# One kernel, one change: the chunks of the mLSTM and of the retention, and the RWKV gram matrices, put out in smaller steps

## The chip, the core and the metric

The kernel runs on one core of one Trainium2 chip. The metric is the device time of one execution in microseconds (us), the median of several runs; the profile shows one further execution, taken by the hardware profiler. Engines are named as in the profile: PE is TensorE (PEld its weight loads), DVE VectorE, ACT ScalarE, POOL GpSimd, and SP the engine whose queue issues the DMA transfers.

## What is computed

One layer over 1024 frames of width 1024, all in float32: an RMS norm, one input projection, three groups of heads side by side, an output projection, a second norm with a SwiGLU feed-forward part, and a last norm.

```python
def reference(x, w_in, ...):
    for l in range(DEPTH):                      # DEPTH = 1
        h = rmsnorm(x, ln1_g[l])
        p = h @ w_in[l]
        pm, pr, pw = jnp.split(p, [M_COLS, M_COLS + R_COLS], axis=-1)
        ym = mlstm_group(pm, ...)               # 4 heads of 64
        yr = retention_group(pr)                # 6 heads of 64
        yw = rwkv7_group(pw, ...)               # 6 heads of 64
        y = jnp.concatenate([ym, yr, yw], axis=-1).astype(x.dtype)
        x = x + y @ w_out[l]
        h = rmsnorm(x, ln2_g[l])
        x = x + (jax.nn.silu(h @ w_gate[l]) * (h @ w_up[l])) @ w_down[l]
    return rmsnorm(x, lnf_g)
```

mLSTM and retention are linear attention with decay, computed chunk by chunk. Within a chunk the scores (keys times queries), weighted by a causal decay mask, multiply the values; the state of the chunks before multiplies the queries; both are added, and the state takes in the chunk's keys and values. RWKV-7 is a recurrence with a delta rule, worked here in blocks of 64 frames: each block needs products of its decayed keys and queries with each other (the gram matrices), the inverse of a triangular matrix, and then a step of a serial chain.

## The kernel before

**Tiling.** Channels lie on 128 partitions, frames in two halves of 512 (h = 0, 1). A float32 projection is made from three products of split operands (a high and a low part, type fp32r), so each weight tile costs three matmuls, 512 frames wide in `three` (L119 to L121) or 256 columns wide in `tok_proj` (L740 to L742). The page calls those results `acc`. Weights come by DMA (`wraw`), and ACT and DVE split them (L90, L93). The small work, in plain float32, uses three PSUM buffers called `misc`; the RWKV chain has two of its own called `chain`.

**The woven stage.** Everything between the input projection and the first half of the output projection is written as Python generators, and `weave` decides in which order their instructions are put out. Each generator yields `(cost, wait)`: the planner's clock moves on by `cost`, and that generator is due again `wait` later; or it yields the name of an event and is due when another generator has signalled it. At each turn the first generator in the list that is due runs up to its next yield. The side work stands first in the list: `rwkv_chain`, `rwkv_inverse`, `rwkv_prep`, `rwkv_out`, `norms`, `attention`. The dense work stands behind: `rwkv_proj`, `fillers`, `out_proj`. So projections fill the time in which no side work is due, in quarters of a tile (`PART`, 1.38 planned us) or halves of a token tile (`TOK` x 256, 1.44). Side work is tied behind the last dense matmul put out before it (`tc.issue_after`); a dense matmul may still be drawn ahead of side work that the compiler's scheduler thinks not ready. PE then takes its instructions in the order that results.

**attention** (L1111 on) runs the eight chunks of 128 frames of the mLSTM, then four and four of the retention, one after another in one generator, each half of retention after its projections (`qkv_r0`, `qkv_r1`). For each chunk it puts out the whole of `mlstm_chunk` (L878) or `ret_chunk` (L947) in one step, then the loads of the next chunk, yields `(4.2, 4.0)` or `(5.0, 4.0)`, puts out the next mLSTM weights (POOL adds the mask at L873, ACT takes four exponentials at L876), stores the retention chunk before (L1007, 0.4 planned us), puts out the normalization of this chunk (`head_norm`), and waits 4.0 more. At the end of a half it signals `mlstm0`, `ret0` and so on; `norms` waits for them before `out_proj` can start on that half.

**A chunk of the mLSTM**: scores (L887), their product with the weights on DVE (L890), state times queries (L896) and weights times values (L898) for each of two head groups q, their sum (L901, L902), transposed keys (L908) scaled on DVE (L910), and the new state (L916, L922).

**A chunk of the retention**: queries and keys transposed (L953) and copied by ACT (L955), scores (L963); for each q the causal mask on DVE (L967, tile `rsw`), state times queries (L973), masked scores times values (L977), a scaling on DVE (L979); then the new state (L986, L989). The store transposes the result (L1007) and splits it.

**The grams** in `rwkv_half`: two passes of 16 matmuls (L466), four blocks each, every pass into two `misc` buffers that DVE empties with three masked products per buffer (L472 to L474). Behind them the step signals `ab` for the triangular inverse and yields `(2.2, 4.0)`.

**The RWKV chain** (L588 to L607) advances 48 blocks one after another, three steps each, with ACT and DVE between them, and ends with a normalization and a transposition (L655).

Of the kernel before, what the change touches and what calls it, by code (L numbers as in the profile page):

```python
# [54 lines left out]
def trunk_kernel(ctx: ExitStack, tc: tile.TileContext, a: dict, out: bass.AP):  # L55
# [16 lines left out]
    def misc_tile():  # L72
        return ps_m.tile([P, HF], F32, name="misc", tag="misc")
# [11 lines left out]
    def cc(name):  # L85
        lo, hi = CST[name]
        return cst[:, lo:hi]
# [101 lines left out]
    def rows_of(q):  # L189
        return slice(q * 64, (q + 1) * 64)  # L190
# [196 lines left out]
    def rwkv_half(i, h, r, k, v):  # L387
# [66 lines left out]
        for q in range(2):  # L454
            rows = rows_of(q)
# [5 lines left out]
        for c0 in range(0, 8, 4):  # L461
            grams = [misc_tile().rearrange("p (c x) -> p c x", c=4) for _ in two]
            for c in range(4):
                for q, g4 in enumerate(grams):
                    rows = rows_of(q)
                    PE.matmul(g4[:, c, :], lhsT=kb[rows, c0 + c, :, :].rearrange("p a t -> p (a t)"),  # L466
                              rhs=E[rows, c0 + c, q, 128:256], start=True, stop=True)
            for q, g4 in enumerate(grams):
                rows, orow = rows_of(q), rows_of(1 - q)
                cs4 = slice(c0, c0 + 4)  # L470
                msk = cc("mask_k").unsqueeze(1).broadcast_to([P, 4, 64])
                V.tensor_tensor(E[orow, cs4, q, 192:256], g4[rows, :, 0:64], msk[rows], ALU.mult)  # L472
                V.tensor_tensor(E[orow, cs4, q, 128:192], g4[orow, :, 0:64], msk[orow], ALU.mult)
                V.tensor_tensor(E[:, cs4, q, 64:128], g4[:, :, 64:128],  # L474
                                cc("mask_r").unsqueeze(1).broadcast_to([P, 4, 64]), ALU.mult)
        dl = sb.tile([P, 8], F32, name="dl", tag="dl", bufs=3)
        G.tensor_copy(dl, er[:, :, 64])
        inv = rwkv_inverse_issue(i, h, E)
        hv_E[i, h] = E, inv
        signal(f"ab{i}{h}", 3.0)  # L480
        yield 2.2, 4.0
        V.tensor_tensor(kb, kb, er[:, :, 64:65].unsqueeze(3).broadcast_to([P, 8, 2, 64]), ALU.mult)
        for c0 in range(0, 8, 4):
            pt = misc_tile()
# [393 lines left out]
    def mlstm_chunk(c, qT, kT, MV, ws):  # L878
        h2, sl = chunk_of(c)
        og = a_tile("og", 256)  # L880
        SY.dma_start(out=og, in_=v_dram[h2][sl, 256:512])
        hh = a_tile("hh", 260).rearrange("p (h d) -> p h d", h=4)
        scores = [misc_tile() for _ in two]
        for p in range(2):
            for q, pss in enumerate(scores):
                rows = rows_of(q)
                PE.matmul(pss[:, p * P:(p + 1) * P], lhsT=kT[rows, p, :], rhs=qT[rows, p, :], start=True, stop=True)  # L887
        for q, pss in enumerate(scores):
            rows = rows_of(q)
            V.scalar_tensor_tensor(ws[q], in0=pss[:, 0:256].rearrange("p (a b) -> p a b", a=2), scalar=0.125, in1=ws[q],  # L890
                                   op0=ALU.mult, op1=ALU.mult)
            po = misc_tile()
            p4 = po[:, 0:260].rearrange("p (w a e) -> p w a e", w=2, a=2)
            if c:
                for p in range(2):
                    PE.matmul(p4[:, 1, p, :], lhsT=qT[rows, p, :], rhs=CS["t"][rows, p, :], start=True, stop=True)  # L896
            for p in range(2):
                PE.matmul(p4[:, 0, p, :], lhsT=ws[q][:, p, :], rhs=MV[:, 2 * p + q, :], start=True, stop=True)  # L898
            dst = hh[:, q::2, :]
            if c:  # L900
                V.tensor_tensor(dst, p4[:, 1], mg["iw"][:, c, q::2].unsqueeze(2).broadcast_to([P, 2, 65]), ALU.mult)  # L901
                V.tensor_tensor(dst, dst, p4[:, 0], ALU.add)  # L902
            else:
                V.tensor_copy(dst, p4[:, 0])
        if c < KT - 1:
            pk = misc_tile()
            for p in range(2):
                PE.transpose(out=pk[:, p * P:(p + 1) * P], in_=kT[:, p, :], identity=ident)  # L908
            ks = a_tile("mks", 256).rearrange("p (h d) -> p h d", d=64)
            V.tensor_tensor(ks, pk[:, 0:256].rearrange("p (h d) -> p h d", d=64),  # L910
                            mg["sw"][:, c, :].unsqueeze(2).broadcast_to([P, 4, 64]), ALU.mult)
            pc = misc_tile()
            p3 = pc[:, 0:130].rearrange("p (a e) -> p a e", a=2)
            for p in range(2):
                for q in range(2):
                    PE.matmul(p3[rows_of(q), p, :], lhsT=ks[:, 2 * p + q, :], rhs=MV[:, 2 * p + q, :], start=True, stop=True)  # L916
            nw = at.tile([P, 2, 65], F32, name="CS", tag="CS", bufs=2)
            if c == 0:
                S.copy(out=nw, in_=p3)
            else:  # L920
                for p in range(2):
                    V.scalar_tensor_tensor(nw[:, p, :], in0=CS["t"][:, p, :], scalar=mg["decr"][:, c, p:p + 1],  # L922
                                           in1=p3[:, p, :], op0=ALU.mult, op1=ALU.add)
            CS["t"] = nw
        return hh, og
# [21 lines left out]
    def ret_chunk(c, qt, kt, RV):  # L947
        h2, sl = chunk_of(c)
        qkT = []
        for z in (qt, kt):  # L950
            pk = misc_tile()
            for p in range(3):
                PE.transpose(out=pk[:, p * P:(p + 1) * P], in_=z[:, p * P:(p + 1) * P], identity=ident)  # L953
            zT = a_tile("rT").rearrange("p (k t) -> p k t", k=3)
            S.copy(out=zT, in_=pk[:, 0:384].rearrange("p (k t) -> p k t", k=3))  # L955
            qkT.append(zT)
        qT, kT = qkT
        y = a_tile("ry").rearrange("p (h d) -> p h d", d=64)
        scores = [misc_tile() for _ in two]
        for p in range(3):  # L960
            for q, pss in enumerate(scores):
                rows = rows_of(q)
                PE.matmul(pss[:, p * P:(p + 1) * P], lhsT=kT[rows, p, :], rhs=qT[rows, p, :], start=True, stop=True)  # L963
        for q, pss in enumerate(scores):
            rows = rows_of(q)
            sw = a_tile("rsw").rearrange("p (a t) -> p a t", a=3)
            V.scalar_tensor_tensor(sw, in0=cc("causal").unsqueeze(1).broadcast_to([P, 3, P]), scalar=1.0,  # L967
                                   in1=pss[:, 0:384].rearrange("p (a j) -> p a j", a=3), op0=ALU.is_lt, op1=ALU.mult)
            po = misc_tile()
            p3 = po[:, 0:192].rearrange("p (a e) -> p a e", a=3)  # L970
            if c:
                for p in range(3):
                    PE.matmul(p3[:, p, :], lhsT=qT[rows, p, :], rhs=RR["t"][rows, p, :], start=(p == 0), stop=False,  # L973
                              skip_group_check=True)
            for p in range(3):
                hd = 2 * p + q
                PE.matmul(p3[:, p, :], lhsT=sw[:, p, :], rhs=RV[:, hd * 64:hd * 64 + 64], start=(c == 0), stop=True,  # L977
                          skip_group_check=True)
            V.tensor_tensor(y[:, q::2, :], p3, cc("qdec")[:, q::2].unsqueeze(2).broadcast_to([P, 3, 64]), ALU.mult)  # L979
        if c < KT - 1:  # L980
            pr = misc_tile()
            p3 = pr[:, 0:192].rearrange("p (a e) -> p a e", a=3)
            for p in range(3):
                for q in range(2):
                    hd = slice((2 * p + q) * 64, (2 * p + q) * 64 + 64)
                    PE.matmul(p3[rows_of(q), p, :], lhsT=kt[:, hd], rhs=RV[:, hd], start=True, stop=True)  # L986
            nw = at.tile([P, 3, 64], F32, name="RR", tag="RR", bufs=2)
            if c:
                V.tensor_tensor(nw, p3, RR["t"], ALU.add)  # L989
                V.tensor_tensor(nw, nw, cc("cdec").unsqueeze(2).broadcast_to([P, 3, 64]), ALU.mult)  # L990
            else:
                V.tensor_tensor(nw, p3, cc("cdec").unsqueeze(2).broadcast_to([P, 3, 64]), ALU.mult)
            RR["t"] = nw
        return (y,)
# [116 lines left out]
    def attention():  # L1111
# [2 lines left out]
                with late(G):  # L1114
                    mlstm_weights(t, args[-1])

        mlstm = ("mlstm", 4.2, mlstm_load, mlstm_chunk, mlstm_finish, None)
        ret = ("ret", 5.0, ret_load, ret_chunk, ret_finish, ret_store)
        for (name, cost, load, chunk, finish, store), start, ts in (
            (mlstm, "qkv_m", range(KT)), (ret, "qkv_r0", range(4)), (ret, "qkv_r1", range(4, KT)),  # L1120
        ):
# [3 lines left out]
            weigh(ts.start, args)  # L1125
            yield 0.0, 2.0
            for t in ts:
                y = chunk(t, *args)
                if t < ts.stop - 1:
                    args = load(t + 1)  # L1130
                yield cost, ATT
# [451 lines left out]
```

## Time and profile before

| What | us |
|---|---|
| median of 3 runs | 1495.96 |
| lowest and highest | 1495.2, 1502.91 |
| the profiled execution | 1500.5 |
| its span, from the first to the last instruction | 1498.7 |
| mean granted clock of PE over the span | 0.961 |

PE is the busiest engine. A page's row of a group gives its line, engine and operation, the tiles written and read, its count, its busy time and the mean of one, and the idle time of that engine in front of it with what ended that. A wait is written `engine line <- releaser: us in total, times, longest`. A matmul's busy time overlaps the next one's, so the distance of two starts tells more of its price than its duration.

### The profile page before, as it was taken

Reading aid. Unit: us, or ns where it says so; the run is one execution under the profiler, and the core shown is the slowest. Engines: PE = TensorE matmul, PEld = TensorE weight load, DVE = VectorE, ACT = ScalarE, POOL = GpSimd, SP = SyncE. Lnnn points to the kernel's source line nnn. Section 1 sums busy time; section 2 is a strip of 40 time slices with the busy share of each in tenths; the row PEclk is TensorE's granted clock in tenths of the full one; section 3 lists DMA queues with packets and bytes.
Section 4 is the critical chain, followed back from the end, with each engine's and each line's share of the span. In section 5 each row is a group of like instructions: output and inputs, shape, how many; then the busy total and the mean of one; then the engine's idle time right before and its main releaser. Section 6 shows DMA issues by size and latency. Waiting matters only on the chain.

```text
span 1498.7 us, 23112 instructions
## 1 busy us (share of the span) xinstructions
PE 1418.3 (95%) x8434; PEld 1152.0 (77%) x8434; DVE 885.4 (59%) x1763; ACT 547.5 (37%) x1179; POOL 436.2 (29%) x539
## 2 busy tenths in 40 slices
PE   7998998989989989999999999999999998999996
PEld 5777777878767878887777888888888887887886
DVE  7458585677756756745478555555555574347334
ACT  7353344223323243234545233333333344224222
POOL 3211122345333232424264443333434420000000
PEclk9999999989988999989999999999999999999998
DMA  5132232343522344463442222222222138336333
GB/s 201 51 131 68 63 100 78 93 118 109 131 66 63 106 119 138 119 184 109 158 169 85 78 85 85 85 85 84 82 69 76 70 128 290 99 95 239 95 98 113
DMA packets 131461, 165.33 MB, mean 110 GB/s; under 512 B 44532, under 2 KB 80532, under 8 KB 130196
## 3 DMA queue, kind: packets, MB, share of 16 engines
q1 hardware_dynamic: 131348, 163.87, 34.7%
q8 instruction: 66, 1.08, 0.3%
q14 instruction: 47, 0.39, 0.1%
HBM read 126.06 MB, written 37.77 MB: 109 GB/s over the span
## 4 chain that ended last, share of the span: by engine, by line
PE 71%; DVE 8%; DMA 8%; issue 3%; POOL 2%; ACT 2%; SPq 1%; DVEq 0%; POOLq 0%; ACTq 0%
PE acc L1193 5%; PE acc L1195 5%; PE acc L1194 5%; PE chain L1383 5%; PE chain L1382 5%; PE chain L1384 5%; PE acc L119 4%; PE misc L1193 4%; PE misc L1195 4%; PE misc L1194 4%; PE acc L121 4%; PE acc L120 3%; PE acc L740 2%; PE acc L741 2%; PE acc L742 2%
## 5 line engine op out<-in xcount | busy, mean ns | idle before, releaser
L93 DVE TENSOR_TENSOR wlo<-wraw,whi 128x512 fp32r<-128x512 f32 (+1 forms) x210 | 148.5, 713 | 138.0 <-ACT whi L90 131.8
L90 ACT ACTIVATE whi<-wraw 128x512 fp32r<-128x512 f32 (+1 forms) x210 | 128.2, 613 | 244.9 <-PE chain L1383 123.5
L90 ACT ACTIVATE whi<-rg 128x512 fp32r<-128x512 f32 x128 | 79.7, 631 | 225.3 <-POOL rg L1254 90.5
L119 PE MATMUL acc<-act,whi 128*128 128x512 f32 x352 | 152.3, 433 | 8.6 <-ACT whi L90 8.4
L740 PE MATMUL acc<-whi,act 128*128 128x256 f32 (+1 forms) x512 | 153.5, 304 | 4.4 <-ACT whi L90 3.9
L93 DVE TENSOR_TENSOR wlo<-rg,whi 128x512 fp32r<-128x512 f32 x128 | 94.5, 739 | 106.6 <-ACT whi L90 106.6
L741 PE MATMUL acc<-wlo,act 128*128 128x256 f32 (+1 forms) x512 | 151.4, 296 | 3.3 <-DVE wlo L93 3.3
L121 PE MATMUL acc<-act,wlo 128*128 128x512 f32 x352 | 146.5, 417 | 2.9 <-DVE wlo L93 2.9
L742 PE MATMUL acc<-whi,act 128*128 128x256 f32 (+1 forms) x512 | 149.3, 292 | 0.0
L1382 PE MATMUL chain<-act,whi 128*128 128x512 f32 (+1 forms) x374 | 144.3, 386 | 3.7 <-ACT act L90 3.7
L120 PE MATMUL acc<-act,whi 128*128 128x512 f32 x352 | 145.4, 414 | 1.4 <-DVE act L258 1.4
L1383 PE MATMUL chain<-act,whi 128*128 128x512 f32 (+1 forms) x374 | 143.9, 385 | 0.5 <-DVE act L93 0.5
L1384 PE MATMUL chain<-act,wlo 128*128 128x512 f32 (+1 forms) x374 | 143.8, 385 | 0.0
L1193 PE MATMUL acc<-act,whi 128*128 128x512 f32 x352 | 140.1, 398 | 2.8 <-ACT pre L1449 2.8
L1194 PE MATMUL acc<-act,whi 128*128 128x512 f32 x352 | 139.4, 396 | 0.0
L1195 PE MATMUL acc<-act,wlo 128*128 128x512 f32 x352 | 139.4, 396 | 0.0
L740 PEld LDWEIGHTS acc<-whi,act 128*128 128x128 f32 x512 | 99.1, 195 | 10.9 <-ACT whi L90 4.7
L741 PEld LDWEIGHTS acc<-wlo,act 128*128 128x128 f32 x512 | 100.1, 195 | 8.4 <-DVE wlo L93 4.5
L1193 PE MATMUL misc<-act,whi 128*128 128x512 f32 x264 | 104.2, 395 | 0.0
L1194 PE MATMUL misc<-act,whi 128*128 128x512 f32 x264 | 103.7, 393 | 0.0
L1195 PE MATMUL misc<-act,wlo 128*128 128x512 f32 x264 | 103.6, 393 | 0.0
L742 PEld LDWEIGHTS acc<-whi,act 128*128 128x128 f32 x512 | 100.0, 195 | 1.6 <-issue 0.3
(326 smaller groups left out, 2825.8 us busy)
## 6 DMA issues: line engine op xcount, KB each, us to landing
wraw<-in_w_down SPq DMA_DIRECT2D x85, 256.0 KB
rg<-in_w_gate SPq DMA_DIRECT2D x22, 512.0 KB
rg<-in_w_up SPq DMA_DIRECT2D x22, 512.0 KB
wraw<-in_w_tm SPq DMA_DIRECT2D x40, 256.0 KB
a_dram<-work SPq DMA_DIRECT2D x39, 256.0 KB
rg<-a_dram SPq DMA_DIRECT2D x9, 1024.0 KB
v_dram<-vt SPq DMA_DIRECT2D x64, 128.0 KB
wraw<-in_w_out SPq DMA_DIRECT2D x32, 256.0 KB
```

The lines of the kernel that those rows point to most:

```text
L90: S.activation(hi, src, AF.Copy, scale=scale)
L93: (eng or V).tensor_tensor(lo, src, hi.bitcast(F32), ALU.subtract)
L119: PE.matmul(ps, lhsT=hi, rhs=xh[:, k, :], start=(k == 0), stop=False)
L740: PE.matmul(o, lhsT=xh[h][:, k, sl], rhs=w[k][0], start=(k == 0), stop=False)
L741: PE.matmul(o, lhsT=xh[h][:, k, sl], rhs=w[k][1], start=False, stop=False)
L742: dense[0] = PE.matmul(o, lhsT=xl[h][:, k, sl], rhs=w[k][0], start=False, stop=(k == KT - 1)).ins
L1193: PE.matmul(ps, lhsT=hi, rhs=hi_x[:, k, :], start=(start and k == 0), stop=False, skip_group_check=True)
L1194: PE.matmul(ps, lhsT=hi, rhs=lo_x[:, k, :], start=False, stop=False, skip_group_check=True)
L1195: PE.matmul(ps, lhsT=lo, rhs=hi_x[:, k, :], start=False, stop=(stop and k == 3), skip_group_check=True)
L1382: PE.matmul(ps, lhsT=hi, rhs=hi_a[:, sl], start=(f == 0), stop=False)
L1383: PE.matmul(ps, lhsT=hi, rhs=lo_a[:, sl], start=False, stop=False)
L1384: PE.matmul(ps, lhsT=lo, rhs=hi_a[:, sl], start=False, stop=(f == FT - 1))
```

## The change

Nothing of the computation changes. `mlstm_chunk` and `ret_chunk` become generators that the attention generator runs with `yield from`: they yield between the scores and the values, before the state, and so on. The planned cost that attention adds after a chunk drops to 1.0. In `ret_chunk` both masked scores are now made before the first product with values. The grams yield once between their two passes. The loads of the next chunk come where they came, after the chunk's last instruction.

```diff
             if c0 == 0:
+                yield 1.1, 0.5
...
-        yield 2.2, 4.0
+        yield 1.1, 4.0
```

In `mlstm_chunk`:

```diff
         for q, pss in enumerate(scores):
-            rows = rows_of(q)
             V.scalar_tensor_tensor(ws[q], in0=pss[:, 0:256].rearrange("p (a b) -> p a b", a=2), scalar=0.125, in1=ws[q],
                                    op0=ALU.mult, op1=ALU.mult)
+        yield 0.8, 1.4
+        for q in range(2):
+            rows = rows_of(q)
             po = misc_tile()
...
         if c < KT - 1:
+            yield 1.8, 0.5
             pk = misc_tile()
...
                             mg["sw"][:, c, :].unsqueeze(2).broadcast_to([P, 4, 64]), ALU.mult)
+            yield 0.3, 1.2
             pc = misc_tile()
```

In `ret_chunk`:

```diff
         qT, kT = qkT
+        yield 0.8, 1.8
         y = a_tile("ry").rearrange("p (h d) -> p h d", d=64)
...
-        for q, pss in enumerate(scores):
-            rows = rows_of(q)
+        sws = []
+        for pss in scores:
             sw = a_tile("rsw").rearrange("p (a t) -> p a t", a=3)
             V.scalar_tensor_tensor(sw, in0=cc("causal").unsqueeze(1).broadcast_to([P, 3, P]), scalar=1.0,
                                    in1=pss[:, 0:384].rearrange("p (a j) -> p a j", a=3), op0=ALU.is_lt, op1=ALU.mult)
+            sws.append(sw)
+        for q, sw in enumerate(sws):
+            yield 1.2, 1.4
+            rows = rows_of(q)
             po = misc_tile()
...
         if c < KT - 1:
+            yield 1.2, 0.5
             pr = misc_tile()
```

In `attention`:

```diff
-        mlstm = ("mlstm", 4.2, mlstm_load, mlstm_chunk, mlstm_finish, None)
-        ret = ("ret", 5.0, ret_load, ret_chunk, ret_finish, ret_store)
+        mlstm = ("mlstm", 1.0, mlstm_load, mlstm_chunk, mlstm_finish, None)
+        ret = ("ret", 1.0, ret_load, ret_chunk, ret_finish, ret_store)
...
-                y = chunk(t, *args)
+                y = yield from chunk(t, *args)
```

More of the change, by code (lines that the diff above doesn't have):

```diff
@@ L475, in rwkv_half @@
                                 cc("mask_r").unsqueeze(1).broadcast_to([P, 4, 64]), ALU.mult)
+            if c0 == 0:
+                yield 1.1, 0.5
         dl = sb.tile([P, 8], F32, name="dl", tag="dl", bufs=3)
```

## The prediction

> **What bounds the kernel now.** I read the page first: the span, the busy shares and the chain that ended last.
>
> ```profile
> span 1498.7 us, 23112 instructions
> PE 1418.3 (95%) x8434; PEld 1152.0 (77%) x8434; DVE 885.4 (59%) x1763; ACT 547.5 (37%) x1179; POOL 436.2 (29%) x539
> PE 71%; DVE 8%; DMA 8%; issue 3%; POOL 2%; ACT 2%; SPq 1%; DVEq 0%; POOLq 0%; ACTq 0%
> ```
>
> TensorE bounds it: 95% busy, 71% of the chain. So an edit is worth what it takes out of PE's idle time, or what it changes in PE's speed. Next, the windows by stage (columns: length, then busy time of PE, PEld, DVE, ACT, POOL, then granted clock).
>
> ```profile
> 0.00:90.00 90.00, 77.81 (x344) 57.49 (x345) 53.87 (x84) 47.34 (x79) 26.93 (x44) 0.98 0.36 125
> 90.00:646.00 556.00, 513.22 (x4168) 426.72 (x4166) 369.61 (x1005) 190.99 (x540) 168.38 (x309) 0.94 0.35 100
> 646.00:746.00 100.00, 97.46 (x727) 74.16 (x728) 49.74 (x103) 46.71 (x126) 36.14 (x45) 0.93 0.45 146
> 746.00:1498.70 752.70, 729.80 (x3201) 593.61 (x3199) 412.19 (x573) 262.44 (x435) 204.74 (x141) 0.98 0.34 111
> ```
>
> The change lives between 90 and 746 us, the woven stage. PE is idle there for 556.0 - 513.2 + 100.0 - 97.5 = 45.3 us, and its clock is 0.94 and 0.93 against 0.98 elsewhere. That is the whole stock. The waits of PE in that stretch say whose it is (columns: total us, times, longest).
>
> ```profile
> PE chain L604 <- ACT X L600: 6.4, 4, 5.3
> PE misc L977 <- DVE rsw L967: 3.9, 2, 2.4
> PE misc L887 <- DMA mq<-mqk_dram: 2.9, 1, 2.9
> PE misc L655 <- POOL yw L851: 2.5, 1, 2.5
> PE misc L466 <- DVE R L528: 1.6, 1, 1.6
> PE misc L466 <- DVE E L474: 1.2, 1, 1.2
> PE misc L973 <- DVE gate L659: 0.8, 1, 0.8
> PE misc L898 <- DVE w L890: 0.6, 1, 0.6
> ```
>
> **Term 1: the waits inside the chunks and grams.** The rows that stand in front of the touched lines are L977, L466 twice, L973 and L898: 3.9 + 1.6 + 1.2 + 0.8 + 0.6 = 8.1 us. L604 and L887 are an RWKV copy and a load; the change moves neither. What such a wait looks like, in the third retention chunk:
>
> ```profile
> 598.53 0.94 PE L963 MATMUL misc<-rT 64*128 64x128 f32 x12
> 599.30 0.78 PE L973 MATMUL misc<-RR,rT 64*128 64x64 f32 x6
> 600.48 0.28 PE L740 MATMUL acc<-whi,act 128*128 128x256 f32 x1
> 602.56 0.55 DVE L967 SCALAR_TENSOR_TENSOR rsw<-cst,misc 128x384 f32<-128x384 f32 x1
> 603.17 0.88 PE L977 MATMUL misc<-rv,rsw 128*128 128x64 f32 x6 [2.41 <-DVE rsw L967]
> 603.98 1.36 PE L973 MATMUL misc<-RR,rT 64*128 64x64 f32 x6
> ```
>
> Scores, a few projection matmuls that slipped in, then PE stands 2.41 us because VectorE, busy with other work, reaches the mask only at 602.56. The change puts 1.2 + 1.4 planned us after the scores of retention and 0.8 + 1.4 after those of the mlstm; the same wait then lies under projection matmuls, a quarter of a tile (1.38 us) or half a token tile (1.44 us) at a time. The grams' second pass needs buffers that VectorE frees (L474); one projection step now stands between the passes. A wait that lasts longer than its cover still shows. I take the 8.1 us as gained; bounds 3 (only the waits up to 1.4 us go: 1.2 + 0.8 + 0.6) and 8.1. A VectorE late by more than that becomes the next wait.
>
> **Term 2: the clock.** Five windows, same columns:
>
> ```profile
> 561.00:573.00 12.00, 10.52 (x91) 9.12 (x88) 7.38 (x18) 3.84 (x13) 4.54 (x7) 0.74 0.69 219
> 597.00:611.00 14.00, 11.59 (x84) 10.42 (x83) 9.17 (x28) 2.69 (x9) 5.81 (x8) 0.76 0.57 163
> 414.00:427.00 13.00, 10.40 (x42) 7.89 (x42) 6.99 (x30) 3.47 (x12) 4.53 (x9) 0.74 0.29 87
> 676.00:684.00 8.00, 8.00 (x74) 6.23 (x73) 3.56 (x9) 3.76 (x10) 3.09 (x3) 1.00 0.50 166
> 443.80:464.20 20.40, 20.40 (x136) 13.11 (x135) 6.58 (x13) 7.13 (x18) 5.26 (x8) 0.50 0.07 20
> ```
>
> Two retention chunks with stalls (561, 597) and the last mlstm chunk (414) run at a mean clock of 0.74 to 0.76; a chunk without a stall (676) keeps 1.00. Lost clock: 12 x 0.26 + 14 x 0.24 + 13 x 0.26 = 9.9 us. Chunks broken up by dense matmuls should keep the clock more often. The fifth window shows that idleness is not needed: PE is busy throughout and yet at 0.50, on small matmuls of the RWKV preparation that the change leaves alone. So I take half, 5 us; bounds 0 and 9.9. The Trainium skill, "TensorE: Matmul & The Clock Gate", Part 1, says that the clock falls to half after an idle window of about 3.4 us. By that rule the 2.41 us stall would not drop it and this term would be 0; the fifth window disagrees with idleness as the only cause.
>
> **Term 3: more switches.** Where PE leaves projections for small matmuls and returns:
>
> ```profile
> 315.88 0.28 PE L742 MATMUL acc<-whi,act 128*128 128x256 f32 x1
> 316.09 0.33 PE L593 MATMUL chain<-pm,E 64*64 64x64 f32 x4
> 316.47 0.38 PE L740 MATMUL acc<-whi,act 128*128 128x256 f32 x1
> 316.69 0.28 PE L741 MATMUL acc<-wlo,act 128*128 128x256 f32 x1
> 316.81 0.29 PE L742 MATMUL acc<-whi,act 128*128 128x256 f32 x1
> ```
>
> Steady starts are 0.12 us apart (316.69 to 316.81); into the small work it is 0.21 and after the return 0.22, so a round trip costs 0.09 + 0.10, about 0.2 us. The change adds one planned break per gram (6), three per mlstm chunk with a state (two of the kind that projections already slipped into, so about 1 x 7), and four per retention chunk, of which the rows at 598 to 604 show that breaks already lie there: I count none. 13 x 0.2 = 2.6 us, less the single matmuls that no longer slip in; I take +2, bounds 0 and 59 x 0.2 = 12 (every new step a new break: 6 + 22 + 31).
>
> **Term 4: loads.** The next chunk's loads are still issued on SP behind the chunk, so now after its last step. To the next mlstm weights (POOL and ACT) that leaves 1.0 + 4.0 planned us in place of 4.2 + 4.0, to the next chunk 9.0 in place of 12.2. But their buffers come free only as the chunk ends, so little real time goes. Behind a late load wait POOL's additions, ACT's exponentials and the RWKV copies queued after those, the 5.3 us of L604. I take +1; bounds 0 and 2.9 (the L887 row once more).
>
> **Term 5: the ends of the retention.** In the planner's numbers a retention chunk grows from 5.0 + 4.0 + 0.4 + 4.0 = 13.4 to 0.8 + 1.8 + 1.2 + 1.4 + 1.2 + 1.4 + 1.2 + 0.5 + 1.0 + 4.0 + 0.4 + 4.0 = 18.9 us; an mlstm chunk from 12.2 to 15.0, which ends 8 x 2.8 = 22 us later, long before retention starts.
>
> ```profile
> L953 PE MATMUL misc<-cst,rq x24: 272/273/421, 557.3 to 693.2; 128*128 128x128 f32 x24
> L1007 PE MATMUL misc<-cst,ry x24: 271/273/328, 592.6 to 712.4; 128*128 128x128 f32 x24
> L607 PE MATMUL chain<-X,E x192: 222/222/369, 163.8 to 735.1; 128*64 128x64 f32 x192
> 692.89 0.55 PE L953 MATMUL misc<-cst,rq 128*128 128x128 f32 x3
> 699.90 0.36 DVE L979 TENSOR_TENSOR ry<-misc,cst 128x192 f32<-128x192 f32 x1 [0.16 <-PE misc L977]
> 704.44 1.00 POOL L846 TENSOR_TENSOR ry<-ry,rg 128x384 f32<-128x384 f32 x1
> ```
>
> Retention (L953 to the last store's L1007) ends at 712.4, the RWKV chain (L607) at 735.1: 22.7 us of slack. Seven chunks x 5.5 = 38.5 us use it up. But the planned waits only order work between projections; with no projection left a chunk runs at its own latency, 692.89 to 700.26 = 7.4 us, plus 5.2 of normalization. Both halves' output projections need it: the first half of retention must end before out_proj can start, the second before the next stage. About one chunk may be left over at either place; alone it costs 12.6 us, with some 6 us of its own PE work (the 8.0 us window at 676 less the projections and chain in it), so a stall of 6.6. I take +2 for both together; bounds 0 and 2 x 6.6 = 13.
>
> **Sum:** -8.1 - 5 + 2 + 1 + 2 = -8.1 us. The profiled execution took 1500.5 us (span 1498.7), 4.5 above the median of 1495.96; its three timed runs reach from 1495.2 to 1502.91. 1500.5 - 8 = 1492.5 there; against the median 1495.96 - 8 = 1488. About 0.5%, 7.5 us, is what a measurement of this kernel can tell from no change.
>
> **Rivals.**
> Slower: the retention becomes the last work. It decides as soon as more than one chunk is left when projections run out. The 38.5 against 22.7 us speak for it, the 7.4 us latency against it. Term 5 is then at its bound, and term 2 at 0, since the stretches without projections are sparse like the fifth window: -8.1 + 2 + 1 + 13 = +8, 1504; with term 1 at its lower bound of 3, +13, 1509.
> The clock takes nothing from the chunks: terms 1, 3, 4, 5 alone, -3 us, 1493. The fifth window speaks for it, and that no wait of a chunk is longer than 2.4 us; the clean window at 676 against. The page named in term 2 comes to the same time.
> The breaks are there already: projections stand between scores and values in the 598 rows, so the steps repeat what the program order does, 0 us, 1496. Against: PE stands 2.41 us in spite of them.
> More than the sum: the RWKV chain is held up by whole chunks too, and its waits (L604, the clock of 0.94 over 556 us, 33 us lost) shrink: -20 us, 1476.
>
> **How the numbers follow.** Forecast (-4 to -14) 0.40, of which 0.33 beyond 0.5%; more than the sum 0.12; clock takes nothing 0.14; breaks there already 0.12; slower 0.22. Faster 0.33 + 0.12 = 0.45, same 0.07 + 0.14 + 0.12 = 0.33, slower 0.22. The range goes from 3 us below the largest gain to just short of the slower case's far end, 1473 to 1508, and leaves out what lies beyond either; the forecast's own is 1482 to 1492.
>
> **What would show it.** Right: the L977, L466, L973 and L898 waits fall below 2 us together; the clock from 90 to 646 rises above 0.94; the last L1007 comes later than 712.4 but before L607's last. Wrong: L1007's last start beyond L607's, with PE idle ahead of out_proj's k = 2; PE waits on mq or w; the stage's end after 746.

## The result, and the profile after

The change makes the kernel a little slower: a median of 1508.24 us (1492.67 to 1525.08, 20 runs) against 1496.22 (20 runs), a ratio of 1.0061 with an interval of 1.0037 to 1.0085. Run once more, beside the experiments, it came out worse: 1515.0 against 1495.53, 1.0141 (1.01 to 1.0181). The two intervals do not meet: the same change cost 0.8% more the second time, so kernels that did not run side by side can be compared only roughly. The ratios are made of undisturbed runs alone, so they differ from the quotients of the medians. The forecast of 1488 had the wrong sign.

The profiled execution took 1510.1 us, 9.6 more than the one before. The lines of its page that answer to those of before:

```profile
span 1508.3 us, 23082 instructions
PE 1421.5 (94%) x8434; PEld 1155.2 (77%) x8434; DVE 875.7 (58%) x1763; ACT 547.4 (36%) x1179; POOL 430.0 (29%) x539
PE 67%; DVE 8%; DMA 6%; issue 6%; POOL 4%; ACT 2%; SPq 0%; POOLq 0%; DVEq 0%; ACTq 0%
```

PE does the same 8434 matmuls in 3.2 us more of busy time over 9.6 us more of span. In the chain that ended last, PE falls from 71% to 67%, and POOL and "issue" rise from 2 and 3% to 4 and 6%: POOL is where a chunk is normalized. Next the windows by stage of the changed kernel (columns as before), with one more for the seam to the next stage:

```profile
90.00:646.00 556.00, 512.30 (x4195) 425.61 (x4193) 367.99 (x1004) 192.98 (x549) 165.11 (x313) 0.93 0.35 102
646.00:746.00 100.00, 95.07 (x682) 72.93 (x680) 47.31 (x98) 43.57 (x114) 32.37 (x39) 0.87 0.48 153
746.00:760.00 14.00, 7.99 (x32) 6.76 (x32) 4.38 (x10) 1.39 (x3) 6.60 (x6) 0.64 0.26 102
```

The long stretch is as it was: 512.3 busy in place of 513.2, clock 0.93 in place of 0.94, although nearly every broken chunk lies in it. The loss sits behind it: from 646 to 746 the clock falls from 0.93 to 0.87, and the 14 us behind are nearly half idle (7.99 us busy at a clock of 0.64, in the kernel before 12.38 at 1.00). PE's waits of the changed kernel from 90 to 770 us that bear on the forecast:

```profile
PE misc L1019 <- POOL ry L848: 6.8, 2, 4.7
PE misc L902 <- DVE w L891: 4.5, 1, 4.5
PE misc L988 <- DVE rsw L974: 2.9, 3, 1.4
PE misc L922 <- DVE mks L915: 2.0, 2, 1.6
PE misc L466 <- DVE rt L527: 0.8, 1, 0.8
PE misc L466 <- DVE w L891: 0.6, 1, 0.6
```

L988 is the old L977: its waits went from 3.9 to 2.9 us, not to nothing. The gram's (L466) halved, 2.8 to 1.4. The mlstm's (L902, the old L898) grew from 0.6 to 4.5. On top stands a wait that was not there before: the store of a retention chunk (L1019, the old L1007) waits 6.8 us for POOL's normalization. When the retention (L959 to L1019) and the RWKV chain (L609, the old L607) ran:

```profile
L959 PE MATMUL misc<-cst,rq x24: 270/273/476, 562.9 to 738.9; 128*128 128x128 f32 x24
L1019 PE MATMUL misc<-cst,ry x24: 270/373/476, 606.7 to 754.6; 128*128 128x128 f32 x24
L609 PE MATMUL chain<-X,E x192: 222/222/314, 168.2 to 708.1; 128*64 128x64 f32 x192
```

The chain ends 27 us earlier than before (735.1), the retention 42 us later (712.4): the two have changed places, and the retention is now last. The first half of it ends late as well: its fourth chunk is stored at 663.4 us, before at 642.3, while the last projection leaves PE at 635.7, before at 645.4. From there to the chunk's store PE has little but side work. The stretch from 637 to 680 us, first in the kernel before, then in the changed one:

```profile
637.00:680.00 43.00, 42.97 (x409) 34.40 (x407) 20.93 (x49) 19.30 (x59) 13.61 (x22) 0.88 0.58 178
```

```profile
637.00:680.00 43.00, 36.35 (x293) 26.68 (x291) 14.01 (x36) 13.12 (x49) 9.46 (x19) 0.68 0.40 121
```

409 matmuls became 293, at a clock of 0.68. Closer, the changed kernel's 637 to 675 us in four windows:

```profile
637.00:644.00 7.00, 3.92 (x20) 2.50 (x18) 2.59 (x7) 1.31 (x6) 1.37 (x4) 1.00 0.78 230
644.00:658.00 14.00, 14.00 (x149) 11.89 (x147) 3.98 (x11) 3.38 (x11) 2.00 (x5) 0.51 0.50 156
658.00:661.00 3.00, 1.68 (x23) 1.12 (x22) 1.96 (x6) 0.92 (x7) 1.34 (x2) 1.00 0.89 252
661.00:675.00 14.00, 11.76 (x61) 7.53 (x62) 3.10 (x8) 4.43 (x17) 3.13 (x8) 0.51 0.07 27
```

Idle 3.08 us at 637 to 644, then 14 us at half clock with small matmuls one behind the other, a gap, 14 more at half clock. The two stretches lose at most 28 x 0.49 = 13.7 us (12.6 by PE's 25.76 busy us); the kernel before has 10 us at half clock from 637 to 680 in this trace, a loss of 5, and none in its second trace. So against this trace of the kernel before, the stretch has some 8 us more of lost clock and 6.6 us more of idle time.

The idle time from 637 to 644 is one gap of 3.08 us:

```profile
643.56 0.22 PE L549 MATMUL misc<-tq,E 32*32 32x32 f32 x2 [3.08 <-DVE tq L544]
```

What ends it is not the retention. The chain that ended last runs through it as follows (start, duration):

```profile
636.99 4.51 DMA wraw<-in_w_out
641.51 0.64 ACT whi L90
642.18 0.69 DVE wlo L93
642.98 0.45 DVE tq L544
643.78 0.41 PE misc L970 x2
```

A tile of the output projection's weights takes 4.51 us to land, ACT and DVE split it, and only then does DVE transpose `tq` for the triangular inverse. The retention's scores (L970) come behind the first of the inverse's matmuls in PE's order. Behind this gap the half clock begins. The same chain a little later, in order of time:

```profile
651.75 1.47 PE misc L984 x6
653.21 1.47 PE misc L988 x6
654.68 0.41 PE chain L606 x4
655.31 0.64 PE misc L998 x12
...
658.76 0.47 DVE var L846
659.58 1.32 POOL var L852
660.98 0.83 POOL ry L853
662.35 1.00 POOL ry L848
663.40 0.47 PE misc L1019
```

It runs straight through the last chunk of the retention's first half: values, state, normalization on DVE and POOL, store. L984 and L988 take 1.47 us each where the same six matmuls take 0.81 at full clock later in this trace. Only then does out_proj get its retention operand. Out_proj's 192nd matmul (the first half done) starts at 737.5 (before 733.6), the 216th, the first tile of the second half, at 763.6 (745.1), the 384th at 802.9 (792.4). The 10.5 us at the 384th are about the whole difference of the two executions. From the last projection to this point PE takes 167.2 us (635.7 to 802.9) in place of 147.0 (645.4 to 792.4), with 14.0 us idle in place of 6.3 and a clock of 0.88 in place of 0.93. So two places lose: the seam at 637 to 680, and the end of the second half at 746 to 760.

### The profile page after: what moved, and what is told of

Its sections match the earlier page's. It is cut to its first block, busy times and chain, and to the rows that moved or that the text cites. A ratio compares the mean times of both kernels' runs of the same rounds, so it can differ in the third digit from the quotient of the medians.

```text
span 1508.3 us, 23082 instructions
## 1 busy us (share of the span) xinstructions
PE 1421.5 (94%) x8434; PEld 1155.2 (77%) x8434; DVE 875.7 (58%) x1763; ACT 547.4 (36%) x1179; POOL 430.0 (29%) x539
## 4 chain that ended last, share of the span: by engine, by line
PE 67%; DVE 8%; DMA 6%; issue 6%; POOL 4%; ACT 2%; SPq 0%; POOLq 0%; DVEq 0%; ACTq 0%
PE acc L1205 5%; PE acc L1206 5%; PE acc L1207 5%; PE chain L1395 5%; PE chain L1394 5%; PE chain L1396 5%; PE acc L119 4%; PE misc L1206 4%; PE misc L1205 4%; PE misc L1207 4%; PE acc L121 3%; PE acc L120 3%; PE acc L742 2%; PE acc L743 2%; PE acc L744 2%
```

## The experiments

**Which part costs?** Four kernels on one chip (kernel before: 1493.86). In the first the retention runs whole again, written as in the kernel before (these lines are not shown), while mlstm and grams stay split. The diffs are against the changed kernel where nothing else is said.

```diff
-        yield 0.8, 1.8
...
-            yield 1.2, 1.4
...
-            yield 1.2, 0.5
...
-        ret = ("ret", 1.0, ret_load, ret_chunk, ret_finish, ret_store)
+        ret = ("ret", 5.0, ret_load, ret_chunk, ret_finish, ret_store)
```

> The chunk of the retention is put out whole, with its planned cost of 5.0, as before the change; mLSTM and grams stay split. Theory E (the split retention ends last: its last transposed store moved from 712 to 754 us and its planned chunk grew from 13.4 to 18.9): the loss goes, the last L1007-type store is back near 712 us or earlier, time -3 to -8 us against before. Theory S (the smaller steps themselves cost, through more switches of TensorE and a lower clock): about half of the loss stays, +3 to +6 us.

Measured: 1.0044 (1.001 to 1.0078); chain's end 736.6, last store 719.3. The chain is back where it was, and so is the retention; yet some loss stays, which the theory of the retention alone does not give.

The reverse, only the retention split, the mlstm chunk written as in the kernel before:

```diff
-            if c0 == 0:
-                yield 1.1, 0.5
...
-        yield 1.1, 4.0
+        yield 2.2, 4.0
...
-        yield 0.8, 1.4
...
-            yield 1.8, 0.5
...
-            yield 0.3, 1.2
...
-        mlstm = ("mlstm", 1.0, mlstm_load, mlstm_chunk, mlstm_finish, None)
+        mlstm = ("mlstm", 4.2, mlstm_load, mlstm_chunk, mlstm_finish, None)
```

> Only the retention is split; mLSTM chunks and grams are whole as before. Theory E: all of the loss or more, +9 to +15 us against before, with the last retention store at 740 us or later and TensorE waiting for it. Theory S: about half of the loss, +3 to +6 us.

Measured: 1.0016 (0.9989 to 1.0042), last store 743.3, chain's end 695.7. Neither theory gave that: E asked for 9 to 15 us, S for 3 to 6, and 2.4 were measured, with an interval of -1.6 to 6.3. The earlier chain, 40 us here, comes with the split retention, and no gain in time goes with it here. The wait at the store is there in full, in this kernel's line numbers:

```profile
PE misc L1014 <- POOL ry L846: 7.8, 2, 6.2
```

Then the whole change, but with the waits behind a retention chunk cut so that its planned length is 13.4 again, as before the change (`ATT` and `NORM` are the two planned waits of 4.0 us behind a chunk):

```diff
-                yield cost, ATT
+                yield cost, 1.0 if name == "ret" else ATT
...
-                yield 0.0, NORM
+                yield 0.0, 1.5 if name == "ret" else NORM
```

> All steps of the change are kept, but the two planned waits behind a retention chunk are cut from 4.0 + 4.0 to 1.0 + 1.5 us, so that the planned chunk is 13.4 us again. Theory E: the last store is back near 712 us, the loss goes and the gain of the broken-up chunks is left, -3 to -10 us against before. Theory S: nothing changes against the changed kernel, +9 us. A third way: the next chunk's loads, now 3.9 planned us ahead of their use instead of 9.4, come late, and waits on rq or rk appear.

Measured: 0.9958 (0.9926 to 0.9991). The first half's last store moved from 663.4 to 650.0, the second's from 754.2 to 736.3, not to the 712 that theory E expected. With nothing but two planned numbers changed, the slower kernel is faster than the kernel before. And the reverse once more, the kernel before (the diff is against it) with nothing broken and only the longer plan:

```diff
-                yield cost, ATT
+                yield cost, ATT + (5.5 if name == "ret" else 0.0)
```

> The kernel before, nothing split, but the wait behind each retention chunk lengthened by the 5.5 planned us by which the change lengthens it. Theory E: the last store moves to about 750 us and the time rises by about as much as the change's ends cost, +8 to +15 us. Theory S: no change, within 3 us, since nothing is split.

Measured: 1.0049 (1.0022 to 1.0077); first half stored at 659.8, second at 746.9. The longer plan alone costs 0.49%, close to the 0.61% first measured for the change. But its trace does not show the same place of loss. These are its stretches from 637 to 680 and from 735 to 770 us:

```profile
637.00:680.00 43.00, 40.80 (x400) 31.17 (x399) 19.02 (x47) 17.26 (x59) 11.25 (x23) 0.92 0.48 145
735.00:770.00 35.00, 33.68 (x155) 27.17 (x153) 26.14 (x34) 16.12 (x29) 20.52 (x15) 0.90 0.41 147
```

The first half is stored 9 us behind the last projection, not 28. The first stretch is about as good as in the profiled execution of the kernel before (42.97 us busy at 0.88; its second trace has 42.98 at 1.00), the second is better (28.75 at 0.85). So this run shows that the longer plan costs, and leaves open where.

**The other parts, and noise.** Four kernels on another chip (before: 1495.53): the changed kernel and the kernel before again, without an edit, then each of the other two parts alone.

> The changed kernel once more, on the chip on which the parts run, so that they can be compared on one chip. All theories: +0.4 to +0.9% against before.

> The kernel before against itself, on the same chip: a ratio of 1.000, within 0.3%, and a trace of this chip to set beside the parts.

Measured: the changed kernel 1.0141 as told above, beyond the 0.4 to 0.9% expected, the kernel before against itself 0.9999 (0.9972 to 1.0026). The traces of the changed kernel agree in shape: first half stored at 672.8 with projections done at 645.7, 27 us apart (28 in the first).

Only the mlstm split, that is the first kernel above with the grams in one step too:

```diff
-            if c0 == 0:
-                yield 1.1, 0.5
...
-        yield 1.1, 4.0
+        yield 2.2, 4.0
```

> Only the mLSTM chunk is split; retention chunk and grams are whole. The kernel with mLSTM and grams split and the retention whole was 0.44% slower, so one of the two costs. Theory M (the split mLSTM costs: its chunks run until 470 us in place of 413 and crowd the preparation of the third RWKV pair): +4 to +7 us here and nothing from the grams alone. Theory G (the grams cost: each pass put off holds up the triangular inverse and with it the RWKV chain): 0 here within 3 us.

Only the grams in two steps, against the kernel before:

```diff
+            if c0 == 0:
+                yield 1.1, 0.5
...
-        yield 2.2, 4.0
+        yield 1.1, 4.0
```

> Only the grams are put out in two steps; the chunks are whole. Theory G: +4 to +7 us, with the RWKV chain's last step later than 735 us by twice some 2.5 us. Theory M: within 3 us of before.

Measured: mlstm alone 1.0067 (1.0034 to 1.01), grams alone 1.0059 (1.0031 to 1.0088). The prediction had both as nearly free, each of the two theories had one of them so, and both cost more than the retention's own split (1.0016, on another chip). In either the last token projection leaves PE at 658.4 us, in the kernel before on that chip at 650.0. With the grams alone the chain ends at 747.2 in place of 735.2, and PE waits longer in it for the copy that ACT makes of `pm`, 11.6 us where the kernel before has 0.8 on the same chip:

```profile
PE chain L595 <- ACT pm L592: 11.6, 5, 5.6
```

The last gram's two passes stood far apart there, with a whole retention chunk between them (start, duration):

```profile
606.53 1.16 PE L466 MATMUL misc<-E,kb 64*128 64x128 f32 x8
607.62 0.55 PE L955 MATMUL misc<-cst,rq 128*128 128x128 f32 x3
...
614.15 0.57 PE L988 MATMUL misc<-rv,rk 128*64 128x64 f32 x12
...
615.58 1.16 PE L466 MATMUL misc<-E,kb 64*128 64x128 f32 x16
```

The inverse waits for the second pass and the chain for the inverse. That became a theory to test: the intruder between the passes is the cost.

**Which end of the retention?** On one chip (before: 1494.04). The short waits of above in the first half of the retention only, then in the second only:

```diff
+                yield cost, 1.0 if name == "ret" and t < 4 else ATT
...
+                yield 0.0, 1.5 if name == "ret" and t < 4 else NORM
```

> The change, with the two waits behind a chunk cut to 1.0 and 1.5 us for the first half of the retention alone (chunks 0 to 3). Theory seam (the loss sits between the last token projection and the output projection of the first half, 637 to 680 us, where PE waits for the first half's retention at a granted clock of 0.68): most of the loss goes, between -4 and +4 us against before. Theory end (it sits behind the last projection, 735 to 770 us): the loss stays, +8 us or more.

The other one:

```diff
+                yield cost, 1.0 if name == "ret" and t > 3 else ATT
...
+                yield 0.0, 1.5 if name == "ret" and t > 3 else NORM
```

> The same cut for the second half alone (chunks 4 to 7). Theory seam: the clock in 637 to 680 us stays near 0.7 and most of the loss stays, +6 us or more against before. Theory end: most of it goes, between -4 and +4 us.

Measured: first half 0.9999 (0.997 to 1.0028), second half 1.0071 (1.0047 to 1.0096). The stretch from 637 to 680 us, first half short, then second half short:

```profile
637.00:680.00 43.00, 43.00 (x405) 33.84 (x404) 24.54 (x51) 23.08 (x66) 16.70 (x25) 1.00 0.56 174
```

```profile
637.00:680.00 43.00, 37.57 (x306) 27.41 (x306) 14.49 (x38) 14.09 (x51) 9.90 (x19) 0.64 0.39 123
```

The short first half alone restores PE to 43.00 of 43.00 at a clock of 1.00 and wins the change's loss back. The short second half alone leaves the seam as in the changed kernel, and the time with it, although the last store comes earlier, at 749.4 (754.2). In the first one the last store came at 739.1, without being asked to: the second half cannot begin before the first has ended. From 735 to 770 us the two hardly differ (29.57 us busy and 29.99, both at 0.85), so of the two places it is the seam that tells them apart. The gap behind the load of output weights stands at the seam of both traces of the changed kernel and of the one with the second half short (3.1, 3.2 and 2.8 us at L549), and not in the one with the first half short. How much of the loss is that load and how much the bare chunk, no run separates: with the retention alone split the first half is stored 19 us behind the last projection as well (656.1 and 636.9), but there that gap is missing, the stretch has 39.52 us busy at 0.92, and the 0.16% measured is not clear of no change.

Then the kernel with the retention alone split, short waits in both halves (against that kernel):

```diff
-                yield cost, ATT
+                yield cost, 1.0 if name == "ret" else ATT
...
-                yield 0.0, NORM
+                yield 0.0, 1.5 if name == "ret" else NORM
```

> Only the retention is split, with the short waits behind a chunk; mLSTM chunks and grams whole as before. If the three parts add up (all split with short waits -0.42%, mLSTM and grams alone +0.44%): -0.8%, about -12 us, the fastest so far. If mLSTM and grams cost only where the retention is whole: the same as with all of them split, -0.4%.

Measured: 0.9949 (0.9925 to 0.9972), 1485.26 us: faster than the kernel before and than the changed one, the fastest of all. That is nearer to the second forecast; the sum of the parts, -0.8%, lies just outside the interval. Both ends are closed (second window: the seam to the next stage, where PE is busy for 28.75 of 35 us in the kernel before and 27.62 in the changed one):

```profile
637.00:680.00 43.00, 43.00 (x351) 33.15 (x350) 24.55 (x52) 22.58 (x65) 13.31 (x21) 1.00 0.46 145
735.00:770.00 35.00, 35.00 (x153) 28.42 (x152) 28.36 (x31) 19.71 (x32) 19.64 (x14) 1.00 0.40 135
```

The same idea for the mlstm, alone split, its waits cut so that a planned chunk is 12.2 again (against the kernel with the mlstm alone):

```diff
-                yield cost, ATT
+                yield cost, 2.6 if name == "mlstm" else ATT
...
-                yield 0.0, NORM
+                yield 0.0, 2.6 if name == "mlstm" else NORM
```

> Only the mLSTM is split, and its waits behind a chunk are cut from 4.0 + 4.0 to 2.6 + 2.6 us, so that the planned chunk is 12.2 us as before. If the loss of the split mLSTM (+0.67% alone) comes from its longer planned chunk: it goes, within 3 us of before. If it comes from the steps themselves (loads, weights, more returns to the projections): it stays, +6 to +12 us, or grows, as the loads have even less time.

Measured: 1.0074 (1.0045 to 1.0104). Nothing is won back: what cured the retention is not what ails the mlstm.

**What do mlstm and grams cost?** Four on one chip (before: 1492.02). The grams alone, due again at once, so that nothing planned comes between the passes (against the kernel with the grams alone):

```diff
-                yield 1.1, 0.5
+                yield 1.1, 0.0
```

> Only the grams are split, as in the run before that cost 0.59%, but the wait between the two passes is 0.0 in place of 0.5, so that the planner puts only steps of the chain or the inverse between them and no chunk. Theory intruder (a whole retention chunk of 5 planned us is put between the passes: 604.9 to 615.6 us, and the inverse and the RWKV chain behind it come later): the loss goes, within 3 us of before, chain end back near 735 us. Theory step (the split itself costs): +6 to +9 us as with 0.5.

Measured: 1.0058 (1.0027 to 1.0089). In its trace the last gram's passes lie together (586.8 and 589.3 us), no chunk between, and it is as slow: the intruder alone does not explain it. The chain still ends at 741.2. Where the time goes is only hinted at. From 480 to 645 us the kernel before on the second chip, then the two kernels with the grams alone, with the chunk between and without:

```profile
480.00:645.00 165.00, 152.38 (x1358) 134.98 (x1357) 113.79 (x317) 51.29 (x153) 54.69 (x93) 0.93 0.40 119
```

```profile
480.00:645.00 165.00, 146.45 (x1243) 128.22 (x1241) 100.60 (x265) 49.15 (x143) 55.05 (x84) 0.86 0.36 106
```

```profile
480.00:645.00 165.00, 150.14 (x1308) 134.15 (x1309) 111.70 (x311) 51.13 (x151) 56.15 (x88) 0.88 0.37 114
```

Fewer matmuls get done there, and at a lower clock, 0.86 and 0.88 for 0.93. But these are single executions, and the harmless kernel with one mlstm break, below, shows 0.87 in the same stretch; so this is a lead and not a cause.

The mlstm alone, with the old cost of 4.2 behind the chunk, so that a load keeps its old lead (this and the next against the kernel with the mlstm alone):

```diff
-        mlstm = ("mlstm", 1.0, mlstm_load, mlstm_chunk, mlstm_finish, None)
+        mlstm = ("mlstm", 4.2, mlstm_load, mlstm_chunk, mlstm_finish, None)
```

> Only the mLSTM is split, and the planned cost behind a chunk stays 4.2 in place of 1.0, so that the next chunk's weights come 8.2 planned us behind their loads, as before the change, and not 5.0. Theory load (POOL's mask additions and ACT's exponentials wait for late loads and hold up what stands behind them): the loss of 0.67% goes, within 3 us of before. Theory steps (three more steps per chunk): it stays, +6 us or more.

Measured: 1.0032 (1.0009 to 1.0055), where the kernel without it had 1.0067 on its own chip; the intervals overlap. The lead of the loads may account for half, or the chips for the difference; this edit lengthens the plan as well, so the two are not cleanly apart.

The mlstm alone, broken only between scores and values:

```diff
-            yield 1.8, 0.5
...
-            yield 0.3, 1.2
...
-        mlstm = ("mlstm", 1.0, mlstm_load, mlstm_chunk, mlstm_finish, None)
+        mlstm = ("mlstm", 3.4, mlstm_load, mlstm_chunk, mlstm_finish, None)
```

> Only the mLSTM is split, and only between scores and values; the two breaks ahead of the new state are taken out, and the planned cost behind is 3.4, which makes 4.2 in sum. Theory steps: about a third of the loss, +2 to +4 us, or a small gain, since the waits of the values (L898) go. Theory load: within 3 us of before as well. If it costs all of 10 us, the break between scores and values is the one that does it.

Measured: 1.0001 (0.9976 to 1.0026). The break over which a wait had been measured is free; the two breaks ahead of the state and the lower cost behind the chunk, which leaves a load 5.0 planned us in place of the 7.4 here, are then what costs, as far as runs on two chips can tell. The run before this one, which keeps those breaks and gives a load 8.2, sets the two apart only in part.

Last, the fastest kernel with tighter waits inside the chunk, to bring the store still earlier:

```diff
-        yield 0.8, 1.8
+        yield 0.8, 1.3
...
-            yield 1.2, 1.4
+            yield 1.2, 1.3
```

> The best version so far (only the retention split, short waits behind a chunk, -0.51%) with the waits inside a chunk cut from 1.8 and 1.4 to 1.3 us, just under one projection quarter of 1.38, where 1.4 takes two of them. Theory seam: the last retention store comes some 15 us earlier than 726 us, nearer the chain's end at 700, and the time falls by another 2 to 6 us. Rival: with one quarter less as a cover the waits for the mask come back and nothing is gained.

Measured: 0.9968 (0.9943 to 0.9993), the last store at 731.0 and not before 726.6: no gain. Shorter planned waits inside the chunk did not bring its end forward. Nor did the waits for the mask come back, as the rival had it: 1.3 us in the traces of both kernels. In the kernel it starts from both stretches were full already, so there was little to win there; here the second has 31.49 us busy of 35, at 0.95.

## Why the prediction was wrong

**The step that failed is term 5, the ends of the retention.** It had the plan right, seven chunks 5.5 us longer each, and the slack of 22.7 us too, and then set it aside with "the planned waits only order work between projections". That misses what comes before: while there are projections, the plan decides how many chunks are put out, and each was put out later. The fourth chunk's transposes (L959) started at 635.8 us in place of 618.8, just as the last projection left, so that whole chunk and its store lay bare. The term counted "about one chunk" at either place, 12.6 us at its own latency and 6.6 of them a stall, and took +2 for both. One chunk was left indeed, but from its transposes to its store it took 27.6 us (635.8 to 663.4), not 12.6: a load of output weights and the inverse stood ahead of its scores, and PE then ran at half clock. Against the profiled execution of the kernel before, the stretch from 637 to 680 us has 6.6 us more of idle time and some 8 us more of lost clock, which the term did not count at all. The old length restored in the first half takes the loss away (0.9999, where the same edit in the second half leaves 1.0071 on the same chip), and the longer plan with nothing broken brings one about (1.0049). That the plan's length in the first half is the cause is shown by these runs; the way through the half clock is read from traces, and the last of these runs lost time without it.

**The rival named it, with the wrong end.** "The retention becomes the last work" held: the store ends behind the chain, PE stands up to 4.7 us in front of it, and the loss shows behind 746 us, as the prediction listed for being wrong. Its 1504 to 1509 holds the 1508 first measured, but partly by luck: it counted 3 to 8.1 us of gain from the waits, which did not come, and nearly nothing for mlstm and grams, which cost. And the end that decides is that of the first half, which the rival did not set apart: the second half's short waits alone (1.0071) leave the loss where it was.

**Term 2, the clock, had the wrong sign.** It hoped for -5 from denser chunks. The clock from 90 to 646 us stayed where it was (0.94 to 0.93) and over the whole span fell from 0.961 to 0.955. One reading behind the term was wrong as well. Its fifth window, busy for 20.40 of 20.40 us at 0.50, was to show that idleness is not needed; but it begins at 443.8 us, just behind an idle gap of 3.11 us (439.7 to 442.8, in front of L547). A better case lies elsewhere in the same trace: 655.5 to 665.6 us ran at 0.50 with PE busy for 10.10 of 10.10 us, and in the 10.5 us ahead of it PE was idle for 0.03. The Trainium skill ("TensorE: Matmul & The Clock Gate", Part 1) says that the clock halves after an idle window of about 3.4 us and returns after a busy one of the same length. The first half of that fits the seam, roughly: the half clock from 644 begins just behind the 3.08 us gap. It does not fit the stretch at 655.5 of the kernel before, nor the prediction's own stall of 2.41 us there, which ended at 603.2: from 604.2 to 611.0 us PE ran at 0.50. The second half doesn't fit either: PE is shown busy for 14.00 of 14.00 us at the seam, at 0.51.

**Mlstm and grams, counted as free but for breaks and loads (terms 3 and 4, +2 and +1), failed as well.** Alone they cost 0.67 and 0.59%, some 9 to 10 us each. For the mlstm the cause is narrowed, across chips, to the breaks ahead of the state together with the lower cost behind the chunk; the way stays open. The wait of 4.5 us at L902 in the changed kernel is not it. It stands in the fifth mlstm chunk, whose scores start at 387.9 us; POOL adds the mask only at 394.9, after standing 4.0 us until 393.0 for a load of the triangular inverse (`R`). With the mlstm alone split, the same wait is 1.2 us and the loss is there. Nor are it more switches: counted from the start times between 90 and 746 us, PE leaves an `acc` matmul for a small one 221 times with the mlstm alone split, 213 times in the kernel before on that chip, and at term 3's 0.2 us that is 1.6 us. In the changed kernel the count fell, 196 against 212. For the grams the cause stays open: the pass that was torn apart is not enough, and what else the later due time moves in the order of everything behind it was not isolated. Whether the parts add up can't be said: 0.16, 0.67 and 0.59% come to 1.4, the whole measured 0.61 and 1.41, and mlstm and grams together 0.44 (0.10 to 0.78), where the two alone make 1.26.

**Term 1, the waits inside the chunks, was mis-sized.** Of its 8.1 us, 1.0 went at the masked scores, 1.4 at the grams and 0.8 at L973, which no longer shows; 3.9 came at the mlstm's weights and 2.0 at the new break ahead of its state (L922). That is 2.7 us more waiting, not 8.1 less. Such rows vary between two traces of one kernel: in the second trace of the kernel before, the mlstm's weights stand at 2.7 us and not 0.6.

**What was right:** "more than the sum" supposed that the chain is held up by whole chunks. It is: with the retention split it ends 19 to 40 us earlier in every trace, while the longer plan alone gives 12 (722.7 us). The kernel with the split retention and the plan kept at its length is 0.5% faster; that this gain is the chain's was not isolated.

## What to carry to other kernels

In this kernel the plan mattered more than the breaks. When a piece of side work is broken into steps in a planned order, add up its planned length before and after, and keep it by shortening the waits around it, above all ahead of a point where dense work runs out and something waits for the piece's end. Break only where a wait is measured. Then look for the loss not where the edit is but at the next place where the dense work is short.

## What the runs showed of the hardware

Time follows the granted clock from run to run. Over the 132 runs of the kernel before on the experiments' chips, each listed with its mean clock (0.954 to 0.972), a hundredth of clock goes with 11.5 us, and what is left scatters by 2.5 us. By that slope 19 of the 21 us that the changed kernel lost on the second chip, mean against mean, go with its clock, 0.9455 against 0.9616; 0.9455 lies outside the range that gave the slope. That is a reading of listed numbers and no proof of cause. Within the traces of the two kernels the clock is one or one half, and the windows that show 0.68 or 0.64 are mixtures. Behind a gap of 3.08 us lay 14 us at half clock, with PE busy throughout, which lose 6.9 us more.
